# Seven products of quarter blocks in place of eight in the first MLP layer of a hybrid transformer layer

## The chip, the cores and the metric

The kernel runs on one core of one Trainium2 chip. The metric is the device time of one execution in microseconds (us). Before the change it is 1320.42 us, the median of three runs (1318.79 to 1323.58). The engines are named as in the profile: PE is TensorE, the matrix engine (PEld its weight load); DVE is VectorE, ACT ScalarE, POOL GpSimd, and SP the engine that issues most transfers.

## The reference

The reference is one layer over 512 latent tokens of width 1024 with 256 context tokens: two parallel mixers, then an MLP with squared ReLU. Only the MLP is touched by the change:

```python
def _sq_relu_mlp(h, w1, w2):
    return jnp.square(jax.nn.relu(h @ w1)) @ w2

x = x + mod_x[5] * _sq_relu_mlp(_modulate(_rms(x, norm_mlp[l]), mod_x[3], mod_x[4]), w_mlp_in[l], w_mlp_out[l])
```

`w1` is 1024 x 4096 and `w2` 4096 x 1024, all in float32.

## The kernel before, in words

Everything lies transposed: the partition axis holds 128 channels, the free axis the 512 tokens. The width of 1024 is 8 blocks (`kt`), the hidden width of 4096 is 32 chunks of 128.

Float32 products are made of three matmuls in a rounded format that PE multiplies faster. Each operand is split into a high part, rounded by a copy on ACT, and a low part, the remainder, which DVE gets by a subtraction. `mm3` (L183 to L185) adds high x high, high x low and low x high into one PSUM bank. So `h2h` and `h2l` are the two parts of the normed and modulated input of the MLP, `wh` and `wl` those of a weight tile, `ah` and `al` those of a chunk of the hidden layer after the squared ReLU.

A weight chunk of 1024 x 128 comes in two tiles `wf` of 128 x 512 (256 KB each) by SP's queue (L176); `wchunk` casts each on ACT (L177) and subtracts on DVE (L178). There are four buffers for `wf`, three for `wh` and three for `wl`.

The MLP runs in four quarters (`qt`). In each, the first layer makes eight chunks of the hidden layer: per chunk 8 blocks x 3 matmuls of 512 columns into a bank `d`. Then `squared_relu` takes the ReLU out of PSUM on ACT (L1250), squares it on ACT for the high part (L1251) and on POOL in full (L1252), and DVE subtracts for the low part (L1253). The second layer then runs over the 8 outputs (`ot`): 8 x 3 matmuls over the quarter's chunks, and DVE adds the result to `x1`, the residual (L1291). The quarter `qt == 0` starts with four chunks in two halves of 256 tokens, whose split weights are kept in tiles `kh` and `kl` (KEEP = 4, eight buffers each), and also finishes a modulation vector (`gemv_step`, `gemv_end`).

The order of the work on each engine is set when the program is built: a scheduler places the instructions by the order of the program text and a timeline of its own, and each engine then works through its list in order. Waits between engines come from tiles: an instruction that reads a tile waits for its writer, one that writes a buffer anew waits for the readers of the tile that was there. How far ahead an engine may run is therefore set by the number of buffers.

Of the kernel before, what the change touches and what calls it, by code (L numbers as in the profile page):

```python
# [7 lines left out]
F32 = mybir.dt.float32  # L8
F32R = mybir.dt.float32r
AF = mybir.ActivationFunctionType  # L10
ALU = mybir.AluOpType
# [4 lines left out]
P = 128  # L16
LOW = 1000000
AHEAD = 100
KT = 8
NL = 512  # L20
NC = 256
# [4 lines left out]
KEEP = 4  # L26
# [51 lines left out]
def f32(ap):  # L78
    return ap.bitcast(F32)
# [3 lines left out]
def tile_layer(ctx, tc, I, out, stop=None, dbg=None):  # L83
    nc = tc.nc
    act = nc.scalar
    dve = nc.vector
    pool = nc.gpsimd
    pe = nc.tensor
# [5 lines left out]
    wp = ctx.enter_context(tc.tile_pool(name="wp", bufs=2, reuse_waits="tile", side="right"))  # L94
# [5 lines left out]
    def bank(tag):  # L100
        return ps.tile([P, 512], F32, tag=tag, name=tag, bufs=banks[tag])
# [60 lines left out]
    WN = 512  # L162
# [19 lines left out]
    def mm3(po, lh, ll, rh, rl, first, last):  # L182
        pe.matmul(po, lh, rh, start=first, stop=False)  # L183
        pe.matmul(po, lh, rl, start=False, stop=False)  # L184
        pe.matmul(po, ll, rh, start=False, stop=last)  # L185

    def split_sb(full, hi, lo):
        act.copy(hi, full)
        dve.tensor_tensor(lo, full, f32(hi), ALU.subtract)
# [19 lines left out]
    def gemv_step(q, acc, kt, ws):  # L209

        n = 1024 // len(ws)
        sc = silc[:, kt, 0:1]
        for i, w in enumerate(ws):
            c = slice(n * i, n * i + n)
            nc.sync.dma_start(w, I["w_mod"][q - 2, kt][:, c])
            if kt == 0:
                dve.tensor_scalar(acc[:, c], w, sc, None, op0=ALU.mult)
            else:
                dve.scalar_tensor_tensor(acc[:, c], w, sc, acc[:, c], ALU.mult, ALU.add)  # L219
# [153 lines left out]
    with tc.tile_pool(name="gt", bufs=1, reuse_waits="tile", side="right") as gt:  # L373
# [29 lines left out]
        for n, dst in ((("le", "ge"), egc), (("gt", "lt"), ekd), (("ones", "ones"), egl)):  # L403
            for d in range(2):
                po = bank("c")[:, :96]
# [15 lines left out]
    for b0, n in ((0, 4), (4, 2)):  # L421
        t = bank("t")[:, :128 * n]
# [722 lines left out]
    def kept():  # L1145
        return [wk.tile([P, WN], F32, tag=t, name="wm", bufs=2 * KEEP) for t in ("kh", "kl")]
# [101 lines left out]
    with tc.tile_pool(name="ml", bufs=1, reuse_waits="tile") as ml:  # L1248
        def squared_relu(po, r, a_, hi, lo):
            act.activation(r, po, AF.Relu)  # L1250
            act.activation(hi, r, AF.Square)  # L1251
            pool.tensor_tensor(a_, r, r, ALU.mult)  # L1252
            dve.tensor_tensor(lo, a_, f32(hi), ALU.subtract)  # L1253

        for qt in range(4):
            ah, al = [], []
            if qt == 0:
                ws = [wchunk(I["w_mi"][f], keep=wk) for f in range(KEEP)]
                for f in range(KEEP):
                    ah.append(ml.tile([P, NL], F32R, tag="ah", name="ah", bufs=16))  # L1260
                    al.append(ml.tile([P, NL], F32R, tag="al", name="al", bufs=16))
                for c, tags in zip(halves, ("ddpp", "cctd")):
                    pos = [bank(t)[:, 0:NC] for t in tags]
                    for kt in range(KT):
                        for po, w in zip(pos, ws):
                            mm3(po, *w[kt], h2h[:, kt, c], h2l[:, kt, c], kt == 0, kt == KT - 1)
                    for f, po in enumerate(pos):
                        r = ml.tile([P, NL], F32, tag="r", name="r", bufs=2)
                        a_ = ml.tile([P, NL], F32, tag="a", name="a", bufs=2)
                        squared_relu(po, r[:, c], a_[:, c], ah[f][:, c], al[f][:, c])  # L1270
            for f in range(len(ah), 8):
                w = wchunk(I["w_mi"][8 * qt + f], eng=pool if qt == 0 and f < KEEP + 2 else dve)
                po = product(w, h2h, h2l, full)
                r = ml.tile([P, NL], F32, tag="r", name="r", bufs=2)
                a_ = ml.tile([P, NL], F32, tag="a", name="a", bufs=2)
                ah.append(ml.tile([P, NL], F32R, tag="ah", name="ah", bufs=16))
                al.append(ml.tile([P, NL], F32R, tag="al", name="al", bufs=16))
                squared_relu(po, r, a_, ah[f], al[f])
                if qt == 0:
                    if f == KEEP:  # L1280
                        ga = gacc(ml)
                    for kt in range(2 * (f - KEEP), 2 * (f - KEEP) + 2):
                        gemv_step(5, ga, kt, kept())
            for ot in range(KT):
                w = wchunk(I["w_mo"][ot, qt])
                po = bank("d")
                for kt in range(KT):
                    mm3(po, *w[kt], ah[kt], al[kt], kt == 0, kt == KT - 1)
                if qt == 0 and ot == 0:
                    gemv_end(5, ga, "c")  # L1290
                dve.scalar_tensor_tensor(x1[:, ot, :], po, mcol[:, 5, ot, 0:1], x1[:, ot, :], ALU.mult, ALU.add)  # L1291
                if qt == 3 and out is not None:
                    act.dma_start(out[:, ot, :], x1[:, ot, :])
# [100 lines left out]
```

## Time and profile before

| | us |
|---|---|
| median of three runs | 1320.42 |
| the profiled execution | 1319.97 |
| its span, first to last instruction | 1318.2 |
| PE busy | 1249.4 (95%) |
| DVE busy | 855.9 (65%) |
| ACT busy | 651.1 (49%) |
| POOL busy | 262.6 (20%) |

The span is what the trace covers; the execution's own time has 1.8 us more around it. The mean granted clock of PE is 0.984 of full speed. The shares are means over very different stages: the MLP, with which the change has to do, fills the last 350 us or so, and there the shares have to be read from stretches of their own. In the rows of PE, a matmul's duration overlaps the next one's; the pace is the distance between two starts. In the rows of the other engines, a duration includes time in which an instruction has been issued but cannot get at its operands.

### The profile page before, as it was taken

To read this page: it belongs to the slowest core of one execution; us is meant where nothing else is said; L and a number is where in the kernel's file an instruction comes from. 1 tells how busy PE (TensorE), PEld (TensorE's weight loads), DVE (VectorE), ACT (ScalarE), POOL (GpSimd) and SP (SyncE) were. 2 spreads that over 40 slices of the span, in tenths; PEclk is the share of its full clock that TensorE was granted. 3 is DMA by queue.
4 is the path that set the end of the run, shared out by engine and by line. 5 is a ranking of instruction groups with operands and counts; after the bars stand their busy time and mean duration, and the time that the engine had idled before them with its cause. 6 is when DMAs were issued, how large, how long until landed. Compare 5 with 4: busy or idle time off the path is not lost. (4 is left out here: it accounts for less than half of the span.)

```text
span 1318.2 us, 21055 instructions
## 1 busy us (share of the span) xinstructions
PE 1249.4 (95%) x7406; PEld 1090.4 (83%) x7406; DVE 855.9 (65%) x1853; ACT 651.1 (49%) x1670; POOL 262.6 (20%) x369
## 2 busy tenths in 40 slices
PE   5899997988999899999989999999999999999998
PEld 4797876877889788889989998888997888888887
DVE  4655798777788768848678788676885333333332
ACT  4557574546753765366566676223453242242331
POOL 0022424314421431122100011232032010010110
PEclk9999998999999899999999999999999999999999
DMA  9332214440334114542111114766452232322232
GB/s 359 112 114 71 71 56 102 130 96 2 97 105 128 48 65 120 141 146 91 35 49 42 40 45 157 265 213 250 167 183 92 96 100 95 98 97 96 97 111 89
DMA packets 112168, 147.39 MB, mean 112 GB/s; under 512 B 45328, under 2 KB 54592, under 8 KB 111936
## 3 DMA queue, kind: packets, MB, share of 16 engines
q1 hardware_dynamic: 69728, 130.31, 29.8%
q10 hardware_dynamic: 42336, 15.76, 5.0%
q8 instruction: 58, 0.95, 0.3%
q14 instruction: 46, 0.38, 0.1%
HBM read 128.83 MB, written 17.20 MB: 111 GB/s over the span
## 5 line engine op out<-in xcount | busy, mean ns | idle before, releaser
L177 ACT CAST wh<-wf 128x512 fp32r<-128x512 f32 (+2 forms) x292 | 177.2, 610 | 358.5 <-PE d L184 288.4
L178 DVE TENSOR_TENSOR wl<-wf,wh 128x512 fp32r<-128x512 f32 (+2 forms) x268 | 183.4, 688 | 173.1 <-ACT wh L177 166.6
L183 PE MATMUL d<-hTh,wh 128*128 128x512 f32 x384 | 158.6, 413 | 5.8 <-DVE tz L881 3.5
L184 PE MATMUL d<-hTl,wh 128*128 128x512 f32 x384 | 155.6, 406 | 0.0
L185 PE MATMUL d<-hTh,wl 128*128 128x512 f32 x384 | 154.9, 403 | 0.0
L183 PE MATMUL d<-ah,wh 128*128 128x512 f32 x256 | 100.2, 393 | 0.0
L185 PE MATMUL d<-ah,wl 128*128 128x512 f32 x256 | 100.0, 393 | 0.0
L184 PE MATMUL d<-al,wh 128*128 128x512 f32 x256 | 99.3, 390 | 0.0
L183 PEld LDWEIGHTS d<-hTh,wh 128*128 128x128 f32 x384 | 74.7, 195 | 21.4 <-DVE tz L881 3.9
L1252 POOL TENSOR_TENSOR a<-r 128x512 f32<-128x512 f32 (+1 forms) x36 | 37.2, 1034 | 266.9 <-ACT r L1250 260.8
L185 PE MATMUL d<-h2h,wl 128*128 128x512 f32 x224 | 87.5, 390 | 1.7 <-DVE wl L178 1.7
L183 PE MATMUL d<-h2h,wh 128*128 128x512 f32 x224 | 87.3, 390 | 0.0
L184 PE MATMUL d<-h2l,wh 128*128 128x512 f32 x224 | 87.2, 389 | 0.0
L185 PEld LDWEIGHTS d<-hTh,wl 128*128 128x128 f32 x384 | 74.4, 194 | 15.3 <-issue 0.4
L184 PEld LDWEIGHTS d<-hTl,wh 128*128 128x128 f32 x384 | 74.8, 195 | 13.4
L1291 DVE SCALAR_TENSOR_TENSOR x<-d,mcol,x 128x512 f32<-128x512 f32 x32 | 24.0, 751 | 59.6 <-PE d L185 59.6
L178 POOL TENSOR_TENSOR wl<-wf,wh 128x512 fp32r<-128x512 f32 x24 | 35.4, 1476 | 130.7 <-ACT wh L177 130.7
L185 PEld LDWEIGHTS d<-ah,wl 128*128 128x128 f32 x256 | 48.1, 188 | 10.8
L184 PEld LDWEIGHTS d<-al,wh 128*128 128x128 f32 x256 | 48.1, 188 | 10.8
L183 PEld LDWEIGHTS d<-ah,wh 128*128 128x128 f32 x256 | 48.1, 188 | 9.8
L185 PEld LDWEIGHTS d<-h2h,wl 128*128 128x128 f32 x224 | 42.1, 188 | 10.9 <-DVE wl L178 2.1
L184 PEld LDWEIGHTS d<-h2l,wh 128*128 128x128 f32 x224 | 42.1, 188 | 8.8
(540 smaller groups left out, 3385.2 us busy)
## 6 DMA issues: line engine op xcount, KB each, us to landing
wf<-in_w_mi SPq DMA_DIRECT2D x64, 256.0 KB
wf<-in_w_mo SPq DMA_DIRECT2D x64, 256.0 KB
wf<-in_w_qkv SPq DMA_DIRECT2D x48, 256.0 KB
wm<-in_w_mod SPq DMA_DIRECT2D x40, 256.0 KB
wm<-in_w_mod SPq DMA_DIRECT2D x16, 512.0 KB
wf<-in_w_gate SPq DMA_DIRECT2D x32, 256.0 KB
wms<-in_w_mod SPq DMA_DIRECT2D x12, 512.0 KB
wf<-in_w_z SPq DMA_DIRECT2D x16, 256.0 KB
```

The source lines that it names most:

```text
L177: act.copy(wh, wf)
L178: eng.tensor_tensor(wl, wf, f32(wh), ALU.subtract)
L183: pe.matmul(po, lh, rh, start=first, stop=False)
L184: pe.matmul(po, lh, rl, start=False, stop=False)
L185: pe.matmul(po, ll, rh, start=False, stop=last)
L1252: pool.tensor_tensor(a_, r, r, ALU.mult)
L1291: dve.scalar_tensor_tensor(x1[:, ot, :], po, mcol[:, 5, ot, 0:1], x1[:, ot, :], ALU.mult, ALU.add)
```

## The change

Three of the four quarters of the first layer are computed in another way; the first quarter and the second layer stay. Two chunks of outputs (2 x 128) are made together. The input's 1024 channels are cut into two halves of four blocks (`HK = 4`), the tokens into two halves of 256, the outputs into the two chunks. So the product is one of 2 x 2 blocks, and `seven` (a form of Strassen's scheme) makes it of seven block products in place of eight: each is 4 blocks x 3 matmuls of 256 columns, on combinations of the weights (s1 to s4) and of the input (`TB`, four of them).

The combinations of the input are made once, by `quarters`, for one block at each of the first four outputs of the first quarter's second layer: POOL adds high and low parts back together, DVE subtracts, and each result is split. The combinations of the weights are made for every pair, four of them, on POOL (`combine`, L1302); then all seven weight operands are split by ACT (L188) and DVE (L189) into `kh` and `kl`. Intermediate sums stay in PSUM where they can (X and Y are added to in place); ACT copies what is needed apart (`keep_part`, L1321), and DVE makes the four quarters `cs` of the two chunks (L1331, L1340, L1343, L1344). `amounts` then takes the maximum with zero on POOL (L1260), the square on ACT (L1261) and on POOL (L1262), and the low part on DVE (L1263). The buffers of `ah` and `al` go from 16 to 11.

```diff
+        def amounts(c_):
+            a_ = ml.tile([P, NL], F32, tag="a", name="a", bufs=2)
+            hi = ml.tile([P, NL], F32R, tag="ah", name="ah", bufs=11)
+            lo = ml.tile([P, NL], F32R, tag="al", name="al", bufs=11)
+            pool.tensor_scalar(a_, c_, 0.0, None, op0=ALU.max)
+            act.activation(hi, a_, AF.Square)
+            pool.tensor_tensor(a_, a_, a_, ALU.mult)
+            dve.tensor_tensor(lo, a_, f32(hi), ALU.subtract)
+            return hi, lo
+        HK = KT // 2
+        TB = []
+        def quarters(kt):
+            f1, f2 = (ml.tile([P, NL], F32, tag=t, name="hf", bufs=2) for t in "ra")
+            pool.tensor_tensor(f1, f32(h2h[:, kt, :]), f32(h2l[:, kt, :]), ALU.add)
+            pool.tensor_tensor(f2, f32(h2h[:, HK + kt, :]), f32(h2l[:, HK + kt, :]), ALU.add)
+            c0, c1 = halves
+            tb = [ml.tile([P, NC], F32, tag="tb", name="tb", bufs=4) for _ in range(4)]
+            dve.tensor_tensor(tb[0], f1[:, c1], f1[:, c0], ALU.subtract)
...
+            for i, t in enumerate(tb):
+                split_sb(t, TB[i][0][:, kt, :], TB[i][1][:, kt, :])
+        def kept_split(full):
+            hi = wk.tile([P, WN], F32R, tag="kh", name="kh", bufs=2 * KEEP)
+            lo = wk.tile([P, WN], F32R, tag="kl", name="kl", bufs=2 * KEEP)
+            split_sb(full, hi, lo)
+            return hi, lo
+        def seven(src0, src1, last):
+            wa = []
+            for src in (src0, src1):
+                for j in range(2):
+                    t = wp.tile([P, WN], F32, tag="wf", name="wa", bufs=4)
+                    nc.sync.dma_start(t.rearrange("p (k n) -> p k n", k=HK), src[:, HK * j:HK * j + HK])
+                    wa.append(t)
+            a11, a12, a21, a22 = wa
+            def combine(x, y, op):
+                t = ml.tile([P, WN], F32, tag="ws", name="ws", bufs=4)
+                pool.tensor_tensor(t, x, y, op)
+                return t
+            X, Y, V, Z = (bank(t)[:, 0:NC] for t in ("d", "p", "c", last))
+            def mult(po, a, b, first):
+                ahi, alo = kept_split(a)
+                for kt in range(HK):
...
+                    for i, (l_, r_) in enumerate(((ahi, rh), (ahi, rl), (alo, rh))):
+                        pe.matmul(po, l_[:, n], r_, start=first and kt == 0 and i == 0,
+                                  stop=kt == HK - 1 and i == 2, skip_group_check=True)
...
+            mult(X, a11, (0, 0), True)
+            p1 = keep_part(X)
+            s1 = combine(a21, a22, ALU.add)
+            mult(V, a12, (1, 0), True)
+            s2 = combine(s1, a11, ALU.subtract)
+            dve.tensor_tensor(cs[0][:, c0], V, p1, ALU.add)
+            mult(Y, s1, 1, True)
+            p5 = keep_part(Y)
+            s4 = combine(a12, s2, ALU.subtract)
+            mult(X, s2, 2, False)
+            u2 = keep_part(X)
+            mult(Z, a22, 4, True)
+            s3 = combine(a11, a21, ALU.subtract)
+            mult(Y, s4, (1, 1), False)
+            dve.tensor_tensor(cs[0][:, c1], Y, u2, ALU.add)
+            mult(X, s3, 3, False)
+            u3 = keep_part(X)
+            dve.tensor_tensor(cs[1][:, c1], u3, p5, ALU.add)
+            dve.tensor_tensor(cs[1][:, c0], Z, u3, ALU.add)
+            return cs
...
-            for f in range(len(ah), 8):
+            for f in range(len(ah), 8 if qt == 0 else 0):
...
+            for f in range(len(ah), 8, 2):
+                for c_ in seven(I["w_mi"][8 * qt + f], I["w_mi"][8 * qt + f + 1], "te"[f // 2 % 2]):
+                    hi, lo = amounts(c_)
+                    ah.append(hi)
+                    al.append(lo)
             for ot in range(KT):
                 w = wchunk(I["w_mo"][ot, qt])
                 po = bank("d")
                 for kt in range(KT):
                     mm3(po, *w[kt], ah[kt], al[kt], kt == 0, kt == KT - 1)
+                if qt == 0 and ot < HK:
+                    quarters(ot)
```

On POOL nothing but the squares of `squared_relu` stood in the whole MLP after its first chunks; this is what stands at the end of its list before:

```order
L1252 TENSOR_TENSOR a<-r 128x256 x8
L178 TENSOR_TENSOR wl<-wf,wh 128x512
L1252 TENSOR_TENSOR a<-r 128x512 x28
L1389 UNCONDITIONAL_BRANCH
L1389 ISA
```

And this is what stands there now, from the last combinations of a quarter's second pair (`wa_120..`, `ws_120..`) to those of its third (`wa_121..`), with the first pair's `cs_118..` and `cs_120..` that `amounts` reads:

```order
L1302 TENSOR_TENSOR ws_12080<-wa_12011,ws_12059 128x512
L1302 TENSOR_TENSOR ws_12116<-wa_12009,wa_12013 128x512
L1260 TENSOR_SCALAR a_11995<-cs_11861 128x512
L1262 TENSOR_TENSOR a_11995<-a_11995 128x512
L1302 TENSOR_TENSOR ws_12201<-wa_12173,wa_12175 128x512
L1260 TENSOR_SCALAR a_12002<-cs_11862 128x512
L1302 TENSOR_TENSOR ws_12219<-ws_12201,wa_12169 128x512
L1262 TENSOR_TENSOR a_12002<-a_12002 128x512
L1302 TENSOR_TENSOR ws_12240<-wa_12171,ws_12219 128x512
L1302 TENSOR_TENSOR ws_12276<-wa_12169,wa_12173 128x512
```

A pair now brings POOL eight operations where two chunks brought two, and the amounts of one pair stand between the combinations of a later one.

On DVE the end of a second layer and the start of the next quarter's first layer stood like this before, where L178 is a weight split and L1291 the update of `x1`:

```order
L1291 SCALAR_TENSOR_TENSOR x_9887<-d,mcol,x_9887 128x512
L178 TENSOR_TENSOR wl<-wf,wh 128x512 x2
L1291 SCALAR_TENSOR_TENSOR x_9887<-d,mcol,x_9887 128x512
L178 TENSOR_TENSOR wl<-wf,wh 128x512 x3
L1253 TENSOR_TENSOR al<-a,ah 128x512
L178 TENSOR_TENSOR wl<-wf,wh 128x512 x2
L1253 TENSOR_TENSOR al<-a,ah 128x512
```

Now the update is L1392 and the splits of the first pair (`kl` from `wa_118..` and `ws_118..` to `ws_119..`) stand around the last two updates:

```order
L189 TENSOR_TENSOR kl_11864<-wa_11849,kh_11863 128x512
L1392 SCALAR_TENSOR_TENSOR x1_9887<-d_11747,mcol_106,x1_9887 128x512
L178 TENSOR_TENSOR wl_11813<-wf_11811,wh_11812 128x512
L189 TENSOR_TENSOR kl_11884<-wa_11851,kh_11883 128x512
L178 TENSOR_TENSOR wl_11819<-wf_11817,wh_11818 128x512
L1392 SCALAR_TENSOR_TENSOR x1_9887<-d_11785,mcol_106,x1_9887 128x512
L189 TENSOR_TENSOR kl_11903<-ws_11881,kh_11902 128x512
L189 TENSOR_TENSOR kl_11923<-ws_11899,kh_11922 128x512
L189 TENSOR_TENSOR kl_11941<-wa_11855,kh_11940 128x512
L189 TENSOR_TENSOR kl_11959<-ws_11920,kh_11958 128x512
L1392 SCALAR_TENSOR_TENSOR x1_9887<-d_11823,mcol_106,x1_9887 128x512
L189 TENSOR_TENSOR kl_11976<-ws_11956,kh_11975 128x512
```

Six of the first pair's seven splits have moved ahead of the second layer's last update; the seventh and those of the other three pairs follow it.

## Rows read from the trace of the kernel before

**Rows 1.** The page: busy time, share of the span and instructions of each engine.
```profile
PE 1249.4 (95%) x7406; PEld 1090.4 (83%) x7406; DVE 855.9 (65%) x1853; ACT 651.1 (49%) x1670; POOL 262.6 (20%) x369
```

**Rows 2.** The chain that ended last, 1000 us to the end, shares by line.
```profile
by line: PE d L185 32.8%; PE d L183 32.8%; PE d L184 32.6%; PE c L224 0.4%; DVE x L1291 0.2%; issue 0.0%
```

**Rows 3.** MLP stretches: length, busy PE, PEld, DVE, ACT, POOL (count), PEclk, DMA, GB/s.
```profile
1058.00:1101.00 43.00, 43.00 (x191) 35.57 (x190) 16.32 (x24) 18.05 (x31) 8.40 (x8) 1.00 0.30 96
1101.00:1145.00 44.00, 44.00 (x194) 36.13 (x193) 16.25 (x24) 10.29 (x17) 0.00 (x0) 1.00 0.29 96
```

**Rows 4.** PE in order of time, first layer, 512 columns: start, duration, instruction.
```profile
1055.71 0.39 PE L183 MATMUL d<-h2h,wh 128*128 128x512 f32 x1
...
1059.79 0.39 PE L183 MATMUL d<-h2h,wh 128*128 128x512 f32 x1
```

**Rows 5.** PE in order of time, two runs of 256 columns.
```profile
939.83 0.28 PE L185 MATMUL d<-ysh,kl 128*128 128x256 f32 x1
...
942.71 0.28 PE L185 MATMUL d<-ysh,kl 128*128 128x256 f32 x1
...
979.06 0.28 PE L183 MATMUL d<-h2h,kh 128*128 128x256 f32 x1
...
981.33 0.28 PE L185 MATMUL d<-h2h,kl 128*128 128x256 f32 x1
```

**Rows 6.** Instructions by line and shape: count, busy us, mean ns, idle before; one POOL square.
```profile
L177 ACT CAST wh<-wf 128x512 fp32r<-128x512 f32 x264 | 163.1, 621 | 347.8 <-PE d L184 288.4 <-issue 13.6 <-DMA dC<-pt 5.9
L469 ACT COPY raw<-d 128x256 f32<-128x256 f32 x16 | 6.0, 374 | 0.0
L178 DVE TENSOR_TENSOR wl<-wf,wh 128x512 fp32r<-128x512 f32 x116 | 79.6, 689 | 112.0 <-ACT wh L177 112.0
L1308 DVE TENSOR_TENSOR qr<-qr,rsw 128x256 f32<-128x256 f32 x8 | 3.3, 410 | 0.0
L537 POOL MEMSET Sx<- 128x512 f32 x3 | 1.4, 528 | 0.0
L625 POOL COPY off<-A 32x384 f32<-32x384 f32 x16 | 11.7, 729 | 8.4 <-DVE A L597 7.8
L625 POOL COPY off<-A 64x768 f32<-64x768 f32 x8 | 8.0, 1002 | 0.5
...
1058.24 1.05 POOL L1252 TENSOR_TENSOR a<-r 128x512 f32<-128x512 f32 x1 [49.78 <-ACT r L1250]
```

**Rows 7.** POOL and DVE in order of time where they meet.
```profile
856.71 4.72 DVE L219 SCALAR_TENSOR_TENSOR ga<-wm,silc,ga 128x512 f32<-128x512 f32 x7
859.28 3.29 POOL L178 TENSOR_TENSOR wl<-wf,wh 128x512 fp32r<-128x512 f32 x1 [9.41 <-ACT wh L177]
861.35 0.68 DVE L1124 SCALAR_TENSOR_TENSOR yt<-yt,d 128x512 f32<-128x512 f32 x1
...
957.83 1.29 POOL L178 TENSOR_TENSOR wl<-wf,wh 128x512 fp32r<-128x512 f32 x1 [9.51 <-ACT wh L177]
957.96 1.71 DVE L178 TENSOR_TENSOR kl<-wf,kh 128x512 fp32r<-128x512 f32 x1
...
994.01 1.92 POOL L1252 TENSOR_TENSOR a<-r 128x512 f32<-128x512 f32 x1 [1.84 <-ACT r L1250]
994.36 0.68 DVE L178 TENSOR_TENSOR wl<-wf,wh 128x512 fp32r<-128x512 f32 x1
```

**Rows 8.** SP and DVE in order of time: a burst of loads and its first reader.
```profile
974.72 10.15 SPq L215 DMA_DIRECT2D wm<-in_w_mod  x16
977.26 0.49 DVE L217 TENSOR_SCALAR ga<-wm,silc 128x512 f32<-128x512 f32 x1 [1.07 <-DMA wm<-in_w_mod]
...
L176 SPq DMA_DIRECT2D wf<-in_w_mi x64: 327/328/382, 935.8 to 1252.5; - x64
```

**Rows 9.** Busy time in two stretches with waits of PE, columns as in rows 3.
```profile
280.00:288.00 8.00, 5.00 (x41) 4.48 (x39) 4.96 (x14) 1.75 (x5) 0.87 (x2) 1.00 0.94 191
288.00:297.00 9.00, 7.50 (x44) 6.87 (x44) 8.06 (x22) 6.51 (x20) 3.31 (x7) 0.81 0.08 26
```

More of the change, by code (lines that the diff above doesn't have):

```diff
@@ new lines, in tile_layer @@
+        HK = KT // 2
[7 more added lines that the diff above has]
+            dve.tensor_tensor(tb[0], f1[:, c1], f1[:, c0], ALU.subtract)
+            dve.tensor_tensor(tb[1], f2[:, c1], tb[0], ALU.subtract)
+            dve.tensor_tensor(tb[2], f2[:, c1], f1[:, c1], ALU.subtract)
+            dve.tensor_tensor(tb[3], f2[:, c0], tb[1], ALU.subtract)
+            for i, t in enumerate(tb):
+                split_sb(t, TB[i][0][:, kt, :], TB[i][1][:, kt, :])
@@ new lines, in kept_split, with keep_part @@
+        def kept_split(full):
[19 more added lines that the diff above has]
+                for kt in range(HK):
+                    n = slice(128 * kt, 128 * kt + 128)
+                    if isinstance(b, tuple):
+                        rh, rl = h2h[:, HK * b[0] + kt, halves[b[1]]], h2l[:, HK * b[0] + kt, halves[b[1]]]
+                    else:
+                        rh, rl = TB[b - 1][0][:, kt, :], TB[b - 1][1][:, kt, :]
+                    for i, (l_, r_) in enumerate(((ahi, rh), (ahi, rl), (alo, rh))):
+                        pe.matmul(po, l_[:, n], r_, start=first and kt == 0 and i == 0,
+                                  stop=kt == HK - 1 and i == 2, skip_group_check=True)
+            def keep_part(po):
+                t = ml.tile([P, NC], F32, tag="tb", name="part", bufs=4)
+                act.copy(t, po)
+                return t
+            cs = [ml.tile([P, NL], F32, tag="r", name="cs", bufs=2) for _ in range(2)]
+            c0, c1 = halves
+            mult(X, a11, (0, 0), True)
[18 more added lines that the diff above has]
+            return cs
@@ L1255, in tile_layer @@
+        for i in range(4):
+            TB.append([ml.tile([P, HK, NC], F32R, name=f"tb{i}{q}") for q in range(2)])
         for qt in range(4):
@@ L1259, in tile_layer @@
                 for f in range(KEEP):
-                    ah.append(ml.tile([P, NL], F32R, tag="ah", name="ah", bufs=16))
-                    al.append(ml.tile([P, NL], F32R, tag="al", name="al", bufs=16))
+                    ah.append(ml.tile([P, NL], F32R, tag="ah", name="ah", bufs=11))
+                    al.append(ml.tile([P, NL], F32R, tag="al", name="al", bufs=11))
                 for c, tags in zip(halves, ("ddpp", "cctd")):
@@ L1275, in tile_layer @@
                 a_ = ml.tile([P, NL], F32, tag="a", name="a", bufs=2)
-                ah.append(ml.tile([P, NL], F32R, tag="ah", name="ah", bufs=16))
-                al.append(ml.tile([P, NL], F32R, tag="al", name="al", bufs=16))
+                ah.append(ml.tile([P, NL], F32R, tag="ah", name="ah", bufs=11))
+                al.append(ml.tile([P, NL], F32R, tag="al", name="al", bufs=11))
                 squared_relu(po, r, a_, ah[f], al[f])
```

## The prediction

> **What bounds the kernel now.** I read the share of busy time first, then the MLP stage cut into stretches of half a period, then the matrix engine's own instructions in order of time, then the two elementwise engines at the places where they run at once, and last the order of instructions of both kernels. The page gives PE 95% of the span, and in the MLP stage the chain that ended last is almost nothing but the three matmuls of a product [rows 1, 2]: the reader is to see three shares near 33% and nothing else above half a percent. Cut into quarters, PE is busy for the whole of every stretch, while DVE works 16 of 43 us, ACT 18 and POOL 8 [rows 3]. So the stage is bound by the rate at which PE issues matmuls. The duration printed for a matmul (0.39 us) is not that rate, since matmuls overlap; the distance between starts is. For 512 columns, 1055.71 to 1059.79 holds 18 steps, 0.2267 us each [rows 4]. Eight chunks of 24 matmuls make 43.5 us for a quarter of the first layer, and the next 43.5 to 44 us are the second layer's quarter.
>
> **What the change does to PE.** It takes out 3 quarters x 8 chunks x 24 = 576 matmuls of 512 columns: 130.6 us. It puts in 12 pairs x 7 products x 4 blocks x 3 = 1008 matmuls of 256 columns. Two runs of 256 columns show the price: 0.1200 us where `ysh` is multiplied (24 steps from 939.83 to 942.71) and 0.1135 us where `h2h` is (20 steps from 979.06 to 981.33) [rows 5]. So 256 columns cost more than half of 512, and the work is 114.4 to 121.0 us: PE would save 9.6 to 16.2 us, not the eighth of the multiplications that the scheme drops at 512-column prices (16.3 us). The nearer row is the second, since its operands are the same `h2h` and `kh`: 84 x 0.1135 = 9.5 us for a pair (10.1 at the other end). This counts only while PE remains the bound.
>
> **What the other engines get for a pair.** Counted from the order and priced by rows that ran undisturbed [rows 6]: ACT has 7 casts of 0.62, 2 squares taken at the same price and 4 copies out of PSUM of 0.37: 7.1 us. DVE has 7 splits and 2 lower parts of 0.69 and 4 additions of 256 columns at 0.41: 7.9 us. POOL has 4 combinations at 1.29 (its own rows of two different inputs), 2 products at 1.05 and 2 maxima. No maximum on POOL is in the trace: from below it is a fill of the same size, 0.53, from above the two-input 1.29; the nearest rows are its copies, 0.73 for 384 and 1.00 for 768 elements, so I take 0.80 for 512. That makes 8.9 us. Each of the three engines alone fits into PE's 9.5 to 10.1 us.
>
> **Why they don't fit together.** DVE and POOL do not read SBUF at once. At 957.83 POOL starts a subtraction of two SBUF tiles and takes its undisturbed 1.29 us; DVE issues one at 957.96, which takes 1.71 us instead of 0.69 and ends 0.55 us after POOL's. The other way round, at 859.28 POOL's takes 3.29 us: DVE had seven operations on two SBUF tiles running until 861.43, and POOL ends 1.14 us after that. The DVE row at 861.35, which reads one SBUF tile and one PSUM bank, takes its plain 0.68 us beside it [rows 7]. So an operation of DVE on two SBUF tiles and one of POOL take turns. What one costs in the queue is 0.55 (DVE, 512 columns), 1.14 (POOL, two inputs), 0.89 for POOL's square (994.01 to 995.93, against the end of DVE's at 995.04); for the maximum 0.80 less the same start of 0.15, 0.65; for the 256-column addition `u3+p5`, 0.41 less 0.14, 0.27.
>
> The Trainium skill has this as a rule: its page "SBUF — State Buffer" (Who interferes with whom) says that the pair of ports that VectorE shares with GpSimd is an exclusive lock, held for the whole instruction, and that a VectorE instruction with two SBUF inputs contends with a GpSimd instruction that reads SBUF. The trace agrees on the turns; by the page's "whole instruction" the prices would be the undisturbed durations, 15.5 us a pair, where the rows' overlap gives 12.9, and I use both as ends.
>
> Of DVE's operations the seven splits (`wa` or `ws` less `kh`), the two lower parts (`a` less `ah`) and `u3+p5` read two SBUF tiles; the three additions from PSUM don't. In turns a pair takes 4 x 1.14 + 2 x 0.89 + 2 x 0.65 + 9 x 0.55 + 0.27 = 12.9 us; at undisturbed durations 8.9 + 6.2 + 0.4 = 15.5. Either end is above PE's 9.5 to 10.1: the port between DVE and POOL becomes the bound of the first layer.
>
> **A quarter, step by step.** Four pairs are 51.6 us in turns (62.0 undisturbed). In the order of DVE six of the first pair's splits, and with them all four combinations, stand ahead of the last update of x (L1392), so they run beside the second layer before, where POOL is idle and DVE works 16 of 44 us [rows 3]: minus 7.9 (9.3). The last pair's two maxima, squares and lower parts run beside the 36 second-layer matmuls that need only `ah` 0 to 5, 8.2 us: minus 4.2 (5.1). Four weight splits of the next second layer stand among them: plus 2.2 (2.8). That leaves 41.7 (50.4) us of port work between the start and the end of the quarter's products. An operation that finds the port free pays its undisturbed time, one that queues the shorter: I take a third of the way up, 44.6.
>
> The port also stands empty. The combination s1 of a pair needs tiles whose four slots are given back by the last combination of the pair before. SP's issues are 0.33 us each, and the first 256 KB tile of a burst issued at 974.72 let DVE start at 977.26, 2.5 us later [rows 8]; the fourth tile is there 3.5 us after the slot is free. POOL's queue has nothing to do in the first such gap, a maximum and a square (1.5) in the second, two maxima and a square (2.2) in the third, and DVE one split (0.55) in each: 2.95, 1.4 and 0.75 us stay empty, 5.1 together. Turning to the second layer, its third output's weights (three `wh` buffers) can only be cast (0.62) and split (0.69) once the first output has its last `ah`: 1.3 us. So the first layer takes 44.6 + 5.1 + 1.3 = 51.0 us in place of 43.5, 7.5 more, three times: 22.5. The ends are 48.1 and 56.8, so 13.8 to 39.9.
>
> **The four quarters() steps** stand in the first second layer, before its fifth output. POOL gets 8 additions, DVE 16 subtractions and 16 splits of 256 columns, ACT 16 casts (6 us of its idle time, no cost). On the port within the first four outputs, 22 us: 8 x 1.14 + 32 x 0.27 + 8 weight splits x 0.55 = 22.2; undisturbed 8 x 1.29 + 32 x 0.41 + 8 x 0.69 = 29.0. Behind a late weight split waits PE itself. A third of the way up: 24.5, cost 2.5 (0 to 7). Loads cost nothing: as many `w_mi` tiles as before, and DMA is busy for 0.3 of the stage.
>
> **Sum.** The profiled execution has a span of 1318.2 and takes 1319.97 us; the median of the runs is 1320.42, 0.45 above. 1319.97 + 22.5 + 2.5 = 1345. Its own range is 1334 to 1367, and the maximum's two ends (0.53, 1.29; six per quarter on the port) add -5 and +9.
>
> **The rivals.**
> *The saving arrives.* Each engine alone fits into a pair's PE time, and if the queues are so spaced that DVE and POOL seldom meet, PE stays the bound and saves 9.6 to 16.2 us less up to 4 for the quarters: 1304 to 1314, say 1310. For it: the stage's PE has no idle now [rows 3], and POOL's rows of 1.05 us repeat undisturbed beside DVE [rows 6]. Against it: that is 8 POOL operations in 43 us, not 32. It decides if the port is asked for less than 9.5 to 10.1 us per pair, and the count gives 12.9.
> *A draw.* The tight prices hold everywhere and the loads land inside other work: 41.7 + 1.3 = 43.0 against 43.5, with 0 to 7 for the quarters: 1318 to 1327.
> *Worse.* PE's waits of 2 to 3 us between products bring its clock down. In the trace PE works 5.0 of 8 us from 280, and of the next 9 us the granted clock is 0.81 [rows 9], so 3.4 of 9 us passed at 1.2 instead of 2.4 GHz and 1.7 us of work was lost; once for each of 9 pairs that wait is 15 us. With the port at undisturbed durations: 1360 to 1385. Against it: waits under 3 us are in many stages, and the mean granted clock of the span is 0.984.
> That the products aren't replaced as said is excluded by the order: 84 matmuls at L1316 for each pair.
>
> **How the numbers follow.** Forecast 0.60, worse 0.18, draw 0.13, saving 0.09. A measurement here tells some 0.5%, 6.6 us, from no change. Forecast and worse are slower by more (0.78), the draw lies within, the saving is faster. The range leaves out the saving and the upper part of the worse case: 1318 to 1370.
>
> **What would show it.** In the profile after: DVE's splits at L189 with a mean well above 0.69 and POOL's combinations at L1302 above 1.29, each released by the other; PE in the pairs' stretches busy for 0.75 to 0.85 of the time, waiting for `kl`, L189; 50 to 52 us from the first to the last product of a quarter; POOL idle before s1 of the second pair, for a DMA. It is wrong if PE is busy throughout in these stretches, or if the L189 rows keep 0.69 while POOL works, or if PE's starts at 256 columns are far from 0.1135.

## The result, and the profile after

After the change the median is 1334.01 us (four runs, 1330.75 to 1336.51), before it 1319.81 on the same chip: a ratio of 1.0112, 95% interval 1.0078 to 1.0146. The forecast was 1345, slower; it is slower, by 14.2 us in place of 24.6. The profiled execution takes 1330.75 us with a span of 1329.0. The part ahead of the MLP, which the change does not touch, took some 6 us less in it than in the profiled execution of before, so everything below is read from lengths within the MLP.

The page's line of busy times answers to [rows 1]:

```profile
PE 1242.6 (93%) x7838; PEld 1097.7 (83%) x7838; DVE 956.6 (72%) x1969; ACT 676.5 (51%) x1746; POOL 390.8 (29%) x449
```

PE is busy for 6.8 us less (1249.4 before) and still ends later. The length of a quarter is the distance between the first products of two quarters (for the last one, to the end of its last matmul), here in the rows of PE in order of time: start, duration, instruction. First of before:

```profile
1051.60 0.39 PE L183 MATMUL d<-h2h,wh 128*128 128x512 f32 x1
...
1139.11 0.40 PE L183 MATMUL d<-h2h,wh 128*128 128x512 f32 x1
```

And of after:

```profile
1048.25 0.28 PE L1316 MATMUL d<-h2h,kh 128*128 128x256 f32 x1
...
1140.09 0.28 PE L1316 MATMUL d<-h2h,kh 128*128 128x256 f32 x1
...
1152.63 0.28 PE L1316 MATMUL c<-h2h,kh 128*128 128x256 f32 x1
...
1153.99 0.39 PE L1316 MATMUL p<-tb,kh 128*128 128x256 f32 x2
...
1155.41 0.40 PE L1316 MATMUL e<-tb,kh 128*128 128x256 f32 x2
...
1156.13 0.28 PE L1316 MATMUL e<-tb,kh 128*128 128x256 f32 x1
1158.34 0.50 PE L1316 MATMUL d<-tb,kh 128*128 128x256 f32 x2 [1.93 <-ACT part L1321]
...
1232.87 0.28 PE L1316 MATMUL d<-h2h,kh 128*128 128x256 f32 x1
```

A quarter was 87.5 us and is 91.8, 92.8 and 92.3: 14.2 more over three. The 12 matmuls of one product from 1152.63 to 1153.99 give 0.1133 us each; at the forecast 0.1135, PE's work on a quarter's products is 336 x 0.1135 = 38.1 us. The products on `tb`, four of a pair's seven, are a little slower: the 12 from 1153.99 to 1155.41 take 0.118 each. The distances between starts less the price of each matmul give what PE waited: 8.2, 9.1 and 8.7 us per quarter within the products (26.0 in all; before 0.1) and 5.2 us in all in the second layer (1.3). Some 3.6 of the 26.0 are no waits but that slower pace: the run below in which PE is busy throughout its products shows 3.6 too. These two sums, and the length of the three quarters together (262.6 before, 276.8 after), are the measure of the experiments below. The windows of products and of second layer in the third quarter answer to [rows 3] (same columns; the last ten matmuls of the products fall into the second window):

```profile
1140.09:1187.46 47.37, 41.46 (x329) 39.13 (x328) 37.72 (x46) 22.96 (x47) 37.72 (x25) 1.00 0.28 90
1187.46:1232.87 45.41, 44.93 (x202) 36.80 (x201) 22.67 (x33) 13.05 (x23) 10.61 (x8) 1.00 0.28 93
```

DVE and POOL each work 37.7 of 47.4 us where they worked 16.3 and 8.4 of 43; POOL's undisturbed price for the same work was put at 8.9 a pair, 35.6. By line (count, shortest/median/longest ns, first and last start):

```profile
L189 DVE TENSOR_TENSOR kl<-ws,kh x48: 674/878/1572, 1046.1 to 1276.2; 128x512 fp32r<-128x512 f32 x48
L1302 POOL TENSOR_TENSOR ws<-wa x24: 1285/1734/1800, 1044.1 to 1273.8; 128x512 f32<-128x512 f32 x24
L1260 POOL TENSOR_SCALAR a<-cs x24: 1477/1861/1928, 1062.6 to 1285.8; 128x512 f32<-128x512 f32 x24
L1263 DVE TENSOR_TENSOR al<-a,ah x24: 674/1090/1787, 1067.0 to 1289.1; 128x512 fp32r<-128x512 f32 x24
```

The splits and lower parts on DVE, 0.69 undisturbed [rows 6], have medians of 0.88 and 1.09 and run up to 1.79; the combinations on POOL 1.73 for 1.29. What PE then waits for, summed by releaser (us in total, times, longest; PE's matmuls, then its weight loads, whose waits partly overlap the first):

```profile
PE d L1316 <- ACT part L1321: 11.6, 14, 1.9
...
PE d L1316 <- DVE kl L189: 0.9, 3, 0.3
...
PEld d L1316 <- ACT part L1321: 15.4, 15, 2.1
```

Not the split but ACT's copy of a sum out of PSUM ends most waits. Why the copy is late is seen in the engines' rows before the wait of 1.93 us that ended at 1158.34 (brackets: idle before, released by):

```profile
1149.76 2.92 DVE L189 TENSOR_TENSOR kl<-ws,kh 128x512 fp32r<-128x512 f32 x2 [2.00 <-ACT kh L188]
1150.50 1.63 POOL L1302 TENSOR_TENSOR ws<-wa,ws 128x512 f32<-128x512 f32 x1
1152.09 1.74 POOL L1302 TENSOR_TENSOR ws<-wa 128x512 f32<-128x512 f32 x1
1152.61 1.78 DVE L189 TENSOR_TENSOR kl<-wa,kh 128x512 fp32r<-128x512 f32 x1
1154.31 0.41 DVE L1340 TENSOR_TENSOR cs<-p,part 128x256 f32<-128x256 f32 x1
1154.64 1.69 DVE L189 TENSOR_TENSOR kl<-ws,kh 128x512 fp32r<-128x512 f32 x2
1154.81 1.85 POOL L1260 TENSOR_SCALAR a<-cs 128x512 f32<-128x512 f32 x1 [0.97 <-DVE cs L1340]
1156.26 0.68 DVE L189 TENSOR_TENSOR kl<-wa,kh 128x512 fp32r<-128x512 f32 x1
1156.70 0.63 ACT L1261 ACTIVATE ah<-a 128x512 fp32r<-128x512 f32 x1 [0.78 <-POOL a L1260]
1157.40 0.62 ACT L188 CAST kh<-wa 128x512 fp32r<-128x512 f32 x1
1157.92 0.37 ACT L1321 COPY part<-d 128x256 f32<-128x256 f32 x1
```

PE's last matmul before the wait issues at 1156.13. ACT's list has `ah` next, which needs the maximum, which needed `cs`. DVE made `cs` late: the three splits ahead of it took 4.7 us, from 1149.76 on, beside two of POOL's combinations, where three undisturbed ones take 2.1. The copy that PE needs stands two places behind `ah`. ACT works only half the time; it is late because it is in order.

### The profile page after: what moved, and what is told of

It is laid out like the page before. It is cut to its first block, busy times and chain, and to the rows that moved or that the text cites. A ratio compares the mean times of both kernels' runs of the same rounds, so it can differ in the third digit from the quotient of the medians.

```text
span 1329.0 us, 22156 instructions
## 1 busy us (share of the span) xinstructions
PE 1242.6 (93%) x7838; PEld 1097.7 (83%) x7838; DVE 956.6 (72%) x1969; ACT 676.5 (51%) x1746; POOL 390.8 (29%) x449
## 5 line engine op out<-in xcount | busy, mean ns | idle before, releaser
L177 ACT CAST wh<-wf 128x512 fp32r<-128x512 f32 (+2 forms) x244 | 147.0, 607 | 225.1 <-PE d L184 154.2
L178 DVE TENSOR_TENSOR wl<-wf,wh 128x512 fp32r<-128x512 f32 (+2 forms) x220 | 153.7, 704 | 89.8 <-ACT wh L177 83.3
L178 POOL TENSOR_TENSOR wl<-wf,wh 128x512 fp32r<-128x512 f32 x24 | 34.7, 1449 | 131.7 <-ACT wh L177 122.8
L1302 POOL TENSOR_TENSOR ws<-wa 128x512 f32<-128x512 f32 x24 | 37.4, 1557 | 110.4 <-DMA wa<-in_w_mi 94.5
L189 DVE TENSOR_TENSOR kl<-ws,kh 128x512 fp32r<-128x512 f32 x48 | 48.7, 1019 | 25.9 <-ACT kh L188 24.1
L188 ACT CAST kh<-ws 128x512 fp32r<-128x512 f32 x48 | 29.8, 621 | 66.2 <-POOL ws L1302 66.2
L183 PEld LDWEIGHTS d<-ah,wh 128*128 128x128 f32 x256 | 48.1, 188 | 15.6 <-ACT wh L177 4.4
L752 POOL TENSOR_SCALAR_AFFINE_SELECT Em<-A 128x256 f32<-128x256 f32 x48 | 23.5, 495 | 124.7 <-PE c L791 95.1
L1316 PE MATMUL d<-tb,kh 128*128 128x256 f32 x192 | 37.1, 291 | 11.7 <-ACT part L1321 11.6
L573 POOL TENSOR_SCALAR_AFFINE_SELECT rh<-ghi 128x256 fp32r<-128x256 f32 x48 | 29.5, 616 | 62.6 <-PE e L578 56.4
L1392 DVE SCALAR_TENSOR_TENSOR x<-d,mcol,x 128x512 f32<-128x512 f32 x32 | 23.6, 747 | 32.5 <-PE d L185 32.4
```

The costliest lines, as they stand in the source:

```text
L177: act.copy(wh, wf)
L178: eng.tensor_tensor(wl, wf, f32(wh), ALU.subtract)
L573: pool.affine_select(t, bc(f32(src[:, b, 8 * d + h0:8 * d + h0 + 2]).unsqueeze(2), [P, 2, P]), pattern=[[0, 2], [sgn, P]], compare_op=ALU. ...
L752: pool.affine_select(t, src, pattern=[[0, 2], [sgn, P]], compare_op=ALU.is_ge, fill=0.0, base=0, channel_multiplier=-sgn)
L1302: pool.tensor_tensor(t, x, y, op)
L1316: pe.matmul(po, l_[:, n], r_, start=first and kt == 0 and i == 0, stop=kt == HK - 1 and i == 2, skip_group_check=True)
```

## The experiments

Theory A: DVE and POOL take turns at SBUF, and that sets the pace. B: POOL is merely slow. C: the order in ACT's list. D, formed on the way: the loads of the next pair. All times below are medians, with the ratio to before (medians of 1318.8 to 1320.7 beside these runs) and its interval; "product waits" are the sum as above over three quarters (after: 26.0).

**The maximum on ACT.**
```diff
-            pool.tensor_scalar(a_, c_, 0.0, None, op0=ALU.max)
+            act.activation(a_, c_, AF.Relu)
```


> The maximum of amounts() moves from GpSimd (1.86 us each in the changed kernel's profile, eight per quarter) to ScalarE as a Relu; nothing else is edited. A quarter (first product to last second-layer matmul) is 92.3 us in the changed kernel and 87.6 in the one before. If turns at the SBUF port set the pace (theory A), POOL loses 3.7 us of each pair, but a maximum lets some of DVE's work through, so a quarter falls by 2 to 4 us, to about 89. If POOL's own length is all there is (theory B: POOL is simply slow, DVE no matter), 4 x 3.7 us leave its chain and a quarter goes to PE's 82 to 84. If ScalarE's queue is the place (theory C: the copies out of PSUM stand behind casts that wait for combinations), two more Relus there leave the quarter at 91 to 93. Time: A 1323 to 1328, B 1303 to 1308, C 1331 to 1336.


Measured 1341.07, 1.0164 (1.0121 to 1.0207): above all three expectations; product waits 33.0. The interval overlaps that of the changed kernel (1.0078 to 1.0146), so that it is slower than that one is likely and not certain. The maximum on ACT takes 0.63, so POOL loses 1.8 us twice a pair, and nothing is gained. Two windows (columns as in [rows 3]) and PE's row between them show what came on top:

```profile
1178.00:1182.00 4.00, 1.90 (x16) 1.69 (x15) 2.52 (x5) 2.72 (x7) 1.04 (x1) 1.00 0.59 196
1182.00:1186.00 4.00, 3.77 (x19) 3.77 (x20) 3.86 (x6) 2.45 (x6) 3.10 (x3) 0.57 0.03 8
```
```profile
1182.23 0.79 PE L1316 MATMUL d<-tb,kh 128*128 128x256 f32 x2 [2.34 <-ACT part L1321]
```

PE worked 1.9 of 4 us and waited 2.34; then the granted clock is 0.57, so it ran at 1.2 GHz for most of 4 us. The mean of that quarter's products is 0.97. In the changed kernel PE's longest wait here is 1.94 us, and the clock of all five windows from 1048 to 1280 is 1.00.

**Combinations that hardly read.**
```diff
-                pool.tensor_tensor(t, x, y, op)
+                pool.memset(t[:, 0:WN], 0.5)
+                pool.memset(t[:, 0:WN], 0.5)
+                pool.tensor_tensor(t[:, 0:8], x[:, 0:8], y[:, 0:8], op)
```


> Each combination of weights on GpSimd becomes two fills of the whole tile and an addition of 8 columns (about 1.2 to 1.4 us, waits and buffers as before), so POOL works as long but hardly reads SBUF; the values of the combinations are left out, and the output is not the reference's. Theory A (DVE and POOL take turns when both read SBUF): DVE's splits at L189 fall from a mean of 1.02 to 1.08 us to below 0.8, and a quarter from 92.3 to 86 to 88 us: 1313 to 1319 us. Theory B (POOL's length alone) and theory C (ScalarE's queue): the quarter stays at 91 to 93 and the time at 1330 to 1336, and the splits keep their mean only if something else than the port lengthens them.


Measured 1311.06, 0.9945 (0.9926 to 0.9964); product waits 3.6, a quarter 84.0 to 84.5 us, all three 252.5. PE is the bound again, as its window says:

```profile
1136.28:1175.65 39.37, 39.37 (x337) 39.37 (x336) 27.93 (x44) 21.46 (x45) 35.43 (x53) 1.00 0.33 112
```

POOL is busy for 35.4 of 39.4 us, as much as in the changed kernel, so B as a matter of POOL's busy time falls. But the fills wait for no load and ran ahead; the combinations' chain became short too. The last experiment takes that apart.

**The `quarters` steps alone**, with the first layer as before.
```diff
-            for f in range(len(ah), 8 if qt == 0 else 0):
+            for f in range(len(ah), 8):
```


> The combinations of the input are made (quarters() in the first second layer) and not used; all first layers are made as before the change. The prediction's term for them was 2.5 us (0 to 7); the profile of the changed kernel shows 48.8 us for that second layer against 45.4, so 3.4. Expected: the first second layer at 48 to 49 us, the other quarters at 87.5, the time 2 to 4 us above the kernel before. If the 3.4 us belong to the products instead (the scheduler's pull of the first pair into that second layer), it is within 1 us of before.


Measured 1323.87, 1.0031 (1.0013 to 1.0048): some 4 us. The second layer beside them takes 50.1 us in place of 45.4, at a granted clock of 0.97; in the changed kernel it takes 48.75, 3.4 more, at 1.00.

**The copies out of PSUM on DVE.**
```diff
-                act.copy(t, po)
+                dve.tensor_copy(t, po)
```


> The four copies of partial sums out of PSUM per pair go from ScalarE to VectorE; in the changed kernel's profile nearly all waits of TensorE inside the pairs (33 us in all) end with such a copy. Theory C (ScalarE's queue order holds them back): the waits go, a quarter falls from 92.3 to 85 to 88 us, the time to 1312 to 1320. Theory A: the copies wait behind splits on VectorE in place of casts on ScalarE, 4 x 0.4 us more on the engine that is short of time; a quarter of 92 to 95, the time 1333 to 1342.


Measured 1335.94, 1.0131 (1.0105 to 1.0158); product waits 29.1. The releaser named in PE's waits is thus not the cause: copies out of ACT's list are as late in DVE's.

**The amounts off POOL.**
```diff
-            pool.tensor_scalar(a_, c_, 0.0, None, op0=ALU.max)
-            act.activation(hi, a_, AF.Square)
-            pool.tensor_tensor(a_, a_, a_, ALU.mult)
+            dve.scalar_tensor_tensor(a_, c_, 0.0, c_, ALU.max, ALU.mult)
+            act.copy(hi, a_)
```


> The changed kernel with GpSimd out of the amounts: max(c,0)*c in one operation on DVE (two SBUF inputs), the rounding to hi by a copy on ACT, lo on DVE as now; the four combinations of a pair stay on GpSimd. Theory A (turns at the port set the pace): per pair 4 x 1.14 + 11 x 0.55 + 0.27 = 10.9 us of turns in place of 12.9, so 5 to 8 us less per quarter until PE's floor: 1314 to 1320 us. Theory B (GpSimd is merely slow; its own time counts): GpSimd falls to 5.2 us per pair and PE is the bound: 1309 to 1314, as in the run without reading combinations. Theory C (the order of ACT's queue): ACT has as many operations at the same places, about 1334 as the changed kernel.


Measured 1336.03, 1.0126 (1.0104 to 1.0149); product waits 30.7. This falsifies A's arithmetic: turns of 10.9 in place of 12.9 us a pair change nothing. B's 1309 to 1314 for a relieved POOL fails as well. POOL's rows show a pair every 11.8 us, of which 5.7 wait for tiles:

```profile
1158.75 1.74 POOL L1301 TENSOR_TENSOR ws<-wa 128x512 f32<-128x512 f32 x1
1166.21 1.27 POOL L1301 TENSOR_TENSOR ws<-wa 128x512 f32<-128x512 f32 x1 [5.72 <-DMA wa<-in_w_mi]
```

From this came theory D.

**The combinations on DVE.**
```diff
-                pool.tensor_tensor(t, x, y, op)
+                dve.tensor_tensor(t, x, y, op)
```


> The changed kernel with the four combinations of a pair on DVE; maximum and square stay on GpSimd. Theory A: the port has 13 x 0.69 + 0.41 + 2 x 0.89 + 2 x 0.65 = 12.5 us per pair in place of 12.9, or 11.2 if the maximum lets DVE through: 1326 to 1334. Theory B: GpSimd is relieved of 4 x 1.7 us; DVE's own 10.7 us per pair is then the longest, 1320 to 1324.


Measured 1320.11, 1.0002 (0.9988 to 1.0016): level with before, product waits 6.4. DVE works 39.1 of 43.2 us in the products and is slowed much less (`kl<-ws` in the mean 0.74 us in place of 1.00):

```profile
1140.91:1184.15 43.24, 42.33 (x348) 41.55 (x347) 39.06 (x60) 21.50 (x46) 18.27 (x13) 1.00 0.34 116
```

More work on the busier engine is faster by 14 us than the same work on the idle one. That lies below A's range and at the end of B's, whose bound was DVE's own 10.7 us a pair; the products take 43.2 / 4 = 10.8. The three quarters take 260.2 us, 2.4 less than before, and the `quarters` steps take that back.

**Every other pair by seven**, and `quarters` at every second output.
```diff
...
+                if f % 4 == 0:
+                    for g in (f, f + 1):
+                        po = product(wchunk(I["w_mi"][8 * qt + g]), h2h, h2l, full)
...
-                if qt == 0 and ot < HK:
-                    quarters(ot)
+                if qt == 0 and ot % 2 == 0:
+                    quarters(ot // 2)
```


> Seven products for the second and fourth pair of each of the last three quarters only, the first and third pair by eight as before; and the four preparing steps quarters() at every second output of the second layer in place of the first four. PE drops to 43.5 - 2 x 1.4 = 40.7 us per quarter. If turns at the port are the cost (A), a pair by eight gives them slack, PE stays the bound and the quarters cost 0 to 3: 1312 to 1316. If each pair by seven has a fixed price of its own (loads through four slots, ACT's queue; C), (46.4 - 1.1 - 43.5) / 4 = 0.45 us each and the quarters 3.4: about 1326.


Measured 1336.70, 1.0127 (1.0097 to 1.0157); above both expectations; product waits 15.6 for half the pairs. Slack beside the pairs does not help: each pair by seven brings its waits with it.

**No maximum.**
```diff
-            pool.tensor_scalar(a_, c_, 0.0, None, op0=ALU.max)
-            act.activation(hi, a_, AF.Square)
-            pool.tensor_tensor(a_, a_, a_, ALU.mult)
+            act.activation(hi, c_, AF.Square)
+            pool.tensor_tensor(a_, c_, c_, ALU.mult)
```


> The changed kernel without the maximum (the amounts are the squares of c with either sign: that part of the computation is left out); all else as it is. The maximum on GpSimd took 1.86 us at the median where 0.80 was predicted. Theory A with the maximum as a turn of 0.65: six turns per quarter less, 3.9 us, 1322 to 1324. Theory B (GpSimd's own time counts): eight times 1.86 = 14.9 us of GpSimd's 37 of 46 us per quarter go, PE's floor, 1310 to 1315. If the maximum costs nothing since it lies beside other work: 1331 to 1337.


Measured 1339.49, 1.0149 (1.0120 to 1.0179); above all three expectations; product waits 33.2 with a granted clock of 0.97 in all three quarters' products. Removing POOL's longest operation does not help; that it slows the kernel is within the noise of the two intervals. `ah` now waits at the head of ACT's list for DVE's `cs`.

**A second set of slots for the tiles.**
```diff
-                    t = wp.tile([P, WN], F32, tag="wf", name="wa", bufs=4)
+                    t = (ml if two else wp).tile([P, WN], F32, tag="wf", name="wa", bufs=4)
```
(`two` is set for odd pairs; `ah` and `al` get 9 buffers.)


> The changed kernel with a second set of four slots for the tiles of a pair (odd pairs load into tiles of the stage's own pool; ah and al get 9 buffers in place of 11 to make room). Theory D, formed from the run with the amounts off GpSimd (a pair every 11.8 us, of which GpSimd combines for 6.0 and waits 5.7 for the next pair's tiles): the loop from the last combination through the loads to the next first one sets the pace, and two sets cut it. Here GpSimd's own 12.7 us per pair (4 x 1.73, 2 x 1.86, 2 x 1.04), partly beside the second layer, is next: 41 to 43.5 us per quarter's products in place of 46.5, 1317 to 1325. Theory A (turns alone): only what stood empty goes, 1 to 2 us per quarter: 1328 to 1331. Theory C (ACT's queue order): 1334.


Measured 1334.05, 1.0109 (1.0076 to 1.0142); product waits 26.8, at a clock of 0.96 to 0.97. At half speed for some 0.07 of 48 us, PE lost about 1.6 us a quarter to the clock, 4.8 in three, so the waits proper fell to some 22; the sum did not.

**The second set with the amounts off POOL** (both edits).


> The second set of slots together with the amounts on DVE and ACT, so that GpSimd has only four combinations a pair, 6.0 to 6.9 us in turns with DVE as before. Theory D: loads are ahead, GpSimd is under PE's 9.5 us a pair, PE is the bound, products of a quarter 39.4 to 40.5 us in place of 47.5: 1336 - 3 x 7.5 = 1311 to 1316. Theory A: turns of 10.9 us a pair, 43 us a quarter: 1322 to 1326. Theory C: 1334 to 1337, since ACT's queue is as in the run with one set.


Measured 1334.83, 1.0102 (1.0068 to 1.0135); product waits 28.0. D falls as the main cause: the tiles are there, and a quarter is at most 1 us shorter. The granted clock is 0.93 in two of the three quarters' products, so by the same estimate some 7 of the 28 us are clock, and the waits proper are some 21, about as with the second set alone. C's forecast holds here, as it did for each of the two edits alone; it failed where the copies left ACT. ACT's waits in the stretch, and its rows and DVE's around the longest wait of PE (2.71 us until 1163.64):

```profile
ACT ah L1261 <- DVE a L1260: 46.8, 20, 5.2
ACT kh L188 <- POOL ws L1301: 25.1, 15, 5.2
```
```profile
1156.42 1.78 DVE L189 TENSOR_TENSOR kl<-wa,kh 128x512 fp32r<-128x512 f32 x1
1158.13 1.77 DVE L189 TENSOR_TENSOR kl<-ws,kh 128x512 fp32r<-128x512 f32 x1
...
1161.90 0.62 ACT L1261 CAST ah<-a 128x512 fp32r<-128x512 f32 x1 [5.24 <-DVE a L1260]
1162.42 0.61 ACT L188 CAST kh<-wa 128x512 fp32r<-128x512 f32 x1
1162.94 0.64 ACT L1320 COPY part<-d 128x256 f32<-128x256 f32 x2
```

Two splits of 1.78 beside POOL's combinations delay `a`; ACT stands still for 5.2 us in front of it, and the copies behind it make PE wait.

**The combinations on DVE, `quarters` behind the update of x at every second output.**
```diff
-                if qt == 0 and ot < HK:
-                    quarters(ot)
...
                 dve.scalar_tensor_tensor(x1[:, ot, :], po, mcol[:, 5, ot, 0:1], x1[:, ot, :], ALU.mult, ALU.add)
+                if qt == 0 and ot % 2 == 0:
+                    quarters(ot // 2)
```
(beside the combinations on DVE)


> The combinations on DVE (1320.1 before this) and the four quarters() steps behind the update of x of every second output, in place of ahead of it in the first four. The second layer of the first quarter took 50.1 us with quarters() alone against 45.4: the waits there were of PE for a bank that DVE's late update of x holds (1.2) and for casts and splits of weights behind the quarters' ones (2.4). If these go with the order, 2 to 3 us less: 1317 to 1318. If the steps' turns between GpSimd and DVE cost it wherever they stand: 1319 to 1321.


Measured 1319.83, 1.0001 (0.9984 to 1.0017): the place of the steps does not matter. No version here that computes the layer beats the kernel before.

**A long chain without turns.**
```diff
-                pool.tensor_tensor(t, x, y, op)
+                pool.tensor_tensor(t[:, 0:8], x[:, 0:8], y[:, 0:8], op)
+                for _ in range(3):
+                    pool.memset(t[:, 8:WN], 0.5)
```


> The changed kernel with each combination on GpSimd replaced by its first 8 columns and then three fills of the other 504 (the values of the combinations are left out). Unlike the run with two fills ahead of the 8 columns, the fills stand behind the wait for the tiles and take about as long as a combination in turns with DVE: 0.2 + 3 x 0.52 = 1.75 us, so the chain of four combinations stays as long as it was, and only the reading of SBUF goes. Theory A (DVE's splits are slowed by GpSimd's reading, and that sets the pace): DVE's splits go back to about 0.7 to 0.8 us and the time to 1311 to 1318. Theory B (the length of GpSimd's chain and its place in the queues set the pace, the turns don't matter): 1328 to 1336, as the changed kernel. In between: both have a share, in proportion.


Measured 1323.21, 1.0030 (1.0017 to 1.0044): between the two, where the expectation gives both a share. The product waits are 3.9 us, as with the short chain, and the splits are back at their undisturbed median:

```profile
L189 DVE TENSOR_TENSOR kl<-ws,kh x48: 677/692/1530, 1050.6 to 1271.7; 128x512 fp32r<-128x512 f32 x48
L189 DVE TENSOR_TENSOR kl<-wa,kh x36: 679/687/1101, 1042.3 to 1269.3; 128x512 fp32r<-128x512 f32 x36
```

The rest of the time stands at the turn to the second layer (14.0 us of waits there, after 5.2): PE's list has 13 matmuls of the second layer ahead of the last 48 matmuls of the products here (two in the changed kernel, ahead of the last 12), and they waited for a late weight load, which SP issued only when POOL's third combination had given a tile back; the clock then fell in the window of the turn.

```profile
1173.07 0.31 POOL L1302 TENSOR_TENSOR ws<-wa,ws 128x8 f32<-128x8 f32 x1
1173.40 1.28 SPq L176 DMA_DIRECT2D wf<-in_w_mo  x3
1176.25 0.62 ACT L177 CAST wh<-wf 128x512 fp32r<-128x512 f32 x1 [3.19 <-DMA wf<-in_w_mo]
1176.92 0.79 PE L183 MATMUL d<-ah,wh 128*128 128x512 f32 x1 [2.21 <-ACT wh L177]
```
```profile
1176.92:1186.82 9.90, 9.90 (x54) 8.50 (x55) 9.02 (x12) 5.38 (x11) 7.88 (x11) 0.83 0.41 139
```

The length of the three quarters weighs both: 276.8 us in the changed kernel, 263.4 here, 252.5 with the short chain. Of these 24.3 us, 13.4 go with the reading of SBUF by the combinations; the other 10.9 stay, now at the turn. The rows above put them down to the length of POOL's chain, by way of the load slots, and to the other order on PE; no run separates those two. Another limit: some fills of a combination were placed ahead of its wait for the tiles, so its chain was not the old length for every pair.

## Why the prediction was right or wrong, step by step

**PE's own part was right.** 0.1135 us per matmul of 256 columns was forecast, with 0.1200 as the other end; 0.1133 is measured on `h2h` and 0.118 on `tb`. With combinations that hardly read the three quarters take 252.5 us for 262.6 before, 10.1 us less, inside the 9.6 to 16.2. The saving exists; what fails is the first rival's condition, that DVE and POOL seldom meet.

**That they take turns was right**, from three meetings in the trace of before [rows 7]. The rule of the Trainium skill, "SBUF — State Buffer" (Who interferes with whom), also says that GpSimd instructions which only write do not contend with a two-input VectorE instruction. The run with three fills agrees: the splits kept a median of 0.69 us beside 68.0 us of fills.

**The pace as a sum of turns was wrong.** The step "four pairs are 51.6 us in turns", with 44.6 and 5.1 us drawn from it, gave 49.7 us of products in a quarter; measured are 38.1 + 8.7 = 46.8. The turns are there, but a quarter's products are not as long as their sum. The error is one of form, not only of size: taking turns away from the sum (the amounts off POOL) or the empty time of the loads (two sets) should have shortened a quarter by 5 us or more; the lengths moved by less than 1 us either way, though the clock took back up to 2 us of a quarter. What the trace shows in its place is a late combination or split that holds the head of ACT's list. That it was this order, rather than another in-order list, is read from rows and not shown by an experiment: the copies moved to DVE changed nothing. What is shown by runs is that the four combinations on POOL are the cause (with them on DVE the kernel is level with before) and that their reading has 13.4 us of it.

**The maximum was mis-sized**: 0.80 taken, bounds 0.53 to 1.29, 1.48 to 1.93 measured. It cost little, since it holds DVE less than was assumed. The split at 1156.26 took its plain 0.68 beside it, another 1.09:

```profile
1170.55 1.79 POOL L1260 TENSOR_SCALAR a<-cs 128x512 f32<-128x512 f32 x1 [0.49 <-DVE cs L1344]
1170.92 1.09 DVE L189 TENSOR_TENSOR kl<-wa,kh 128x512 fp32r<-128x512 f32 x1
```

The 33 two-input operations of DVE that met only a maximum took 0.67 to 1.10 us, the 23 that met only a combination up to 1.78. The split in these rows also ends (1172.01) before the maximum does (1172.34). From 1048 us on, 18 of DVE's two-input operations start and end inside one of the 24 maxima; none does inside one of the 45 combinations or the 24 squares there. So turns that last for the whole instruction, one end of the prediction's prices, fit the operations of two inputs and not the maximum.

**The turn to the second layer** was put at 1.3 us a quarter; the second layer's waits grew by (5.2 - 1.3) / 3 = 1.3. The size is right, and casts of `wh` are what PE waits for, as was said; but it does so at two places, in the third quarter 0.38 us at 1185.71 and 0.48 at 1199.82.

**The `quarters` steps** were put at 2.5; 3.4 in the changed kernel and some 4 alone, inside the 0 to 7. Of the 3.4, 1.2 is a wait that the prediction did not have: at 1013.26 PE waits for a bank that DVE's late update of x gives back.

**The sum by the trace:** 14.2 + 3.4 = 17.6 us in the MLP against 25.0 forecast; 7.4 too much: 22.5 - 14.2 = 8.3 from the three quarters, nearly all of it the products' 3 x (49.7 - 46.8) = 8.7, less 0.9 from the preparing steps. The medians differ by 14.2 us; the other 3.4 are within what the part ahead of the MLP varies by. That the median lies near the lower end of the prediction's own range (1334 to 1367) is in part luck: the direction rests on turns that are real, the size on a sum that has the wrong form.

**What would show it:** the splits well above 0.69 and combinations above 1.29, yes. PE was to be busy for 0.75 to 0.85, it was 0.875 (41.46 of 47.37), and to wait for `kl`; it waits for `part`. The 50 to 52 us from first to last product were 48.6 (1140.09 to 1188.65). POOL does stand idle before s1 of the second pair, for 5.2 us where 2.95 was put, but the last thing it waits for is DVE's `cs` and not the load:

```profile
1147.79 1.29 POOL L1302 TENSOR_TENSOR ws<-wa 128x512 f32<-128x512 f32 x1 [5.21 <-DVE cs L1331]
```

**The worse case's mechanism is real but was not reached.** Its clock fall does not appear in the changed kernel's MLP. It appears in experiments (0.97 of full speed in the products with the maximum on ACT and without a maximum, 0.96 with two sets, 0.93 with two sets and the amounts off POOL). With the second set it took back part of what the edit gave.

## What to carry to other kernels

An idle engine is not free help if it shares its path to SBUF with the one that feeds the bound: here the four combinations cost 14 us less on the engine that was already the busier. Before an operation is given to GpSimd, count how many two-input DVE operations it will run beside, and then look not at the sum but at which in-order list is stopped by the later of the two, and at which loads wait for the longer chain. A releaser named in a wait is the last link only: move it, and if the wait stays, the cause is further up.

## What the runs showed of the hardware that was not expected

- A maximum with a constant on GpSimd (128x512, one input) takes 1.48 us alone and up to 1.93 beside DVE, longer than an addition of two tiles alone (1.29). DVE's two-input operations took 1.10 at most beside it, 0.4 more than undisturbed, and 18 of them ran from start to end inside a maximum, where none did inside an addition or a product of two inputs.
- Fills on GpSimd (0.52 us) leave DVE's two-input operations undisturbed (0.69 at the median in both runs with fills).
- PE's clock fell to 0.57 over 4 us after a wait of 2.34 us in a stretch where it had worked 1.9 of 4 us. So an edit that makes one wait longer and the others shorter can lose.
